# A hybrid streaming encoder on one core: a planner's table of durations is replaced, and the DeltaNet state update of two heads becomes one full-height matmul

## The chip, the cores and the metric

The kernel runs on one core of one Trainium2 chip. The metric is device time in microseconds (us) of one execution; smaller is better. The engines are named as in the profile: PE (TensorE matmul), PEld (its weight loads), DVE (VectorE), ACT (ScalarE), POOL (GpSimd), SP (SyncE, which issues the DMAs).

## What is computed

Two layers over 2048 prompt frames and 32 sample frames of width 1024. Layer 0 is sliding-window attention (16 query heads, 4 key heads, ALiBi, sinks). Layer 1 is a gated DeltaNet with 8 heads of 128 keys by 128 values, in chunks of 64 frames. Each layer has an input projection, a SiLU gate, an output projection and a residual; RMSNorm stands before each layer and at the end. The change touches the DeltaNet recurrence, which the reference writes as a scan over chunks:

```python
def step(s, xs):
    qi, ki, ui, wi, gi, ai = xs
    v_new = ui - jnp.einsum('bhcd,bhde->bhce', wi, s)
    o = jnp.einsum('bhcd,bhde->bhce', qi * jnp.exp(gi)[..., None], s) + jnp.einsum('bhij,bhje->bhie', ai, v_new)
    g_last = gi[..., -1]
    s = s * jnp.exp(g_last)[..., None, None] + jnp.einsum(
        'bhcd,bhce->bhde', ki * jnp.exp(g_last[..., None] - gi)[..., None], v_new)
    return s, o
```

## The kernel before, in words

**Tiling.** The tokens go through in four slabs of 512 (the second with the 32 sample frames, 544). Both projections are blocks of 24 matmuls (8 slices of the contraction by 3 products of a split into a high and a low part) into a PSUM bank `pj`; 512 columns at a time, or 272 for the slab of 544. They read activations `hk` and weights `wh`. In the profile they are the group pj<-hk,wh.

**The chain.** Heads are worked on in pairs, head x in the partitions of half x (64 frames of a chunk in each half). `chain_quad` (line 1635) does four chunks of a pair; 128 chunk steps for the prompt and 4 for the sample make 132. A step is a sequence over three engines, each part waiting for the one before:
- PE, two matmuls tb<-st,kq: keys and queries of each head times its state `st`;
- DVE, two scalar_tensor_tensor r<-tb,nbk,vb, one for each half; ACT scales the queries' part into `qs` after them, from the same bank;
- PE, tb<-r,btt: the inverse of the chunk's triangle times `r` (tb<-r,kqs in the last pair, and `kqs` stands for `kq` in the sample);
- ACT, a copy of the 128x128 result out of PSUM: `vn`, the new values of both heads, one head in each half of the partitions;
- PE, for each head a matmul of 64 rows, keys `kd` of its half times `vn` of its half, one into the bank tc and one into the free part of the bank tb; then tb<-vn,bit for the output;
- DVE, two scalar_tensor_tensor st<-st,egl: the decayed state plus the update; then `o`.
The next chunk of the pair needs the new `st`. So that PE has work meanwhile, projection matmuls of later blocks stand between the parts of a step.

**What sets the order.** Generators emit the program's operations; an object `Estimate` (line 77), with costs and lags of its own, decides when each generator goes on, so it sets the order of emission. Every operation is recorded by `Engine.made` (line 180; all instructions therefore have line 185 in the profile) with a rank, its place in the emission, less a lead for urgent ones (400 for evacuations of `pj`, 600 for the chain, line 220). Before the attention layer ends and at the program's end `Order.flush` (line 313) plans: it goes through time, and on each engine issues, of the operations that by its own account are ready, the one of lowest rank; if none is ready, the engine waits for the first that will be. An operation's cost there is the one from `Estimate.cost` (line 119), and the lag between engines is `Estimate.LAG` (line 82). The plan is no more than an order: on the chip each engine takes its instructions in that order, and waits where an input is late.

Of the kernel before, what the change touches and what calls it, by code (L numbers as in the profile page):

```python
# [12 lines left out]
F32R = mybir.dt.float32r  # L13
AF = mybir.ActivationFunctionType
ALU = mybir.AluOpType

P = 128
# [5 lines left out]
CH = 64  # L23
# [53 lines left out]
class Estimate:  # L77
# [4 lines left out]
    LAG = {  # L82
        "tensor": {"tensor": 0, "vector": 200, "scalar": 200, "gpsimd": 200},
        "vector": {"tensor": 256, "vector": 127, "scalar": 130, "gpsimd": 155},
        "scalar": {"tensor": 270, "vector": 145, "scalar": 34, "gpsimd": 160},
        "gpsimd": {"tensor": 200, "vector": 60, "scalar": 75, "gpsimd": 100},
    }
    MEAN = 200
# [82 lines left out]
class Engine:  # L171
# [5 lines left out]
    def __getattr__(self, op):  # L177
        call = getattr(self.engine, op)

        def made(*args, **kw):  # L180
            is_ap = lambda x: isinstance(x, bass.AP)
            outs = [x for x in ([] if "out" in kw else [args[0]]) + [kw.get("out"), kw.get("accum_out")] if is_ap(x)]
            ins = [x for x in list(args[0 if "out" in kw else 1 :]) + [v for k, v in kw.items() if k not in ("out", "accum_out")] if is_ap(x)]
            cost = self.est.note(self.name, op, outs, ins, kw)
            self.order.add(Op(self.name, lambda: call(*args, **kw), cost, op == "dma_start"), ins, outs)  # L185

        return made

# [7 lines left out]
class Op:  # L196


    def __init__(self, engine, call=None, cost=0.0, dma=False):
        self.engine, self.call, self.cost, self.dma = engine, call, cost, dma  # L200
        self.after, self.left, self.ends, self.done, self.rank = [], 0, {}, False, 0
        self.gang = None


class Place:
# [6 lines left out]
class Order:  # L212
# [15 lines left out]
    @contextmanager  # L228
    def together(self):

        self.gang = Op(None)
        self.ops.append(self.gang)
        yield
        self.gang = None

    def place(self, pool, tag, bufs, name):
        ring = self.rings.setdefault((id(pool), tag), [])
# [57 lines left out]
    def settle(self, op):  # L295

        if op.engine:
            lag = lambda by: self.est.LAG.get(by, {}).get(op.engine, self.est.MEAN)
            heapq.heappush(self.wait[op.engine], (max([end + lag(by) for by, end in op.ends.items()] + [0.0]), op.rank, op))
        else:  # L300
            self.finish(op)
# [11 lines left out]
    def flush(self):  # L313

        overs = []
        for p in self.places.values():
            if p.old and p.over is None:
                p.over = Op(None)
                overs.append(p.over)
                for o in p.old.ops:  # L320
                    self.link(o, p.over)
                for o in {id(o): o for o in p.ops}.values():
                    self.link(p.over, o)
                    if o.gang:
                        self.link(p.over, o.gang)
        self.wait = {e: [] for e in self.ENGINES}
        ready = {e: [] for e in self.ENGINES}
        for o in [o for o in overs + self.ops if o.left == 0]:
            self.settle(o)
        while any(self.wait.values()) or any(ready.values()):  # L330
            when = {e: max(self.free[e], 0.0 if ready[e] else self.wait[e][0][0]) for e in self.ENGINES if ready[e] or self.wait[e]}
            e = min(when, key=when.get)
            now = when[e]
            while self.wait[e] and self.wait[e][0][0] <= now:
                _, rank, o = heapq.heappop(self.wait[e])
                heapq.heappush(ready[e], (rank, o))
            _, op = heapq.heappop(ready[e])
            op.call()
            if op.dma:
                self.free[e] = now + 60  # L340
                self.dma = max(now + 1500, self.dma) + op.cost * (self.CLOSE if now < self.START else 1)
                op.ends = {"dma": self.dma + 500}
            else:
                self.free[e] = now + op.cost
                op.ends = {e: self.free[e]}
            op.start = now
            self.finish(op)
        assert all(o.done for o in self.ops)
        self.ops = []
# [49 lines left out]
class Kern:  # L399
# [848 lines left out]
    def delta_setup(self, bp):  # L1248
        nc = self.nc
        self.bp = bp  # L1250
        one = lambda shape, tag, dt=F32: self.t(bp, shape, tag, dt, bufs=1)
        self.st = one([P, DNH, P], "st")
        self.hist = one([P, 24, 3], "hist")
        nc.gpsimd.memset(self.hist, 0.0)
        self.hsmp = one([P, 24, 3], "hsmp")
        nc.sync.dma_start(self.hsmp, self.io["cv"])
        self.csmp = one([P, 24, 3], "csmp")

        self.cw = one([P, 96], "cw")
        nc.vector.tensor_scalar(out=self.cw, in0=self.par[:, PC_CW : PC_CW + 96], scalar1=0.5, scalar2=None, op0=ALU.mult)  # L1260
        self.dg = one([P, 1], "dgn")
        nc.vector.tensor_scalar(out=self.dg, in0=self.par[:, PC_DG : PC_DG + 1], scalar1=0.5, scalar2=None, op0=ALU.mult)
        self.na_ = one([P, 4], "na")
        nc.scalar.activation(self.na_, self.par[:, PC_AL : PC_AL + 4], AF.Exp)
        nc.vector.tensor_scalar(out=self.na_, in0=self.na_, scalar1=-1.0, scalar2=None, op0=ALU.mult)

        self.tts = [one([P, 4, P], f"btt{i}") for i in range(2)]
        self.its = [one([P, 4, P], f"bit{i}") for i in range(4)]

        def zeros():  # L1270
            for x in (*self.its, *self.tts, self.st):
                nc.gpsimd.memset(x, 0.0)
                yield 1000

        self.spawn(zeros(), "zeros", 5000)
        self.npair = self.nconv = 0
        self.chained, self.order, self.quads, self.had = set(), [], [], [None, None]
# [357 lines left out]
    def chain_quad(self, q, tab, off, states, gated, put):  # L1635
# [10 lines left out]
        for c in range(m):  # L1646
            state = yield from states(c)
            p1 = yield from self.bank("tb")
            self.issue.lead = Order.CHAIN
            for x in range(2):  # L1650
                self.mm(p1[:, x * P : (x + 1) * P], kq[:, c, x, :], state[:, x, :], True, True)
            r = self.t(bp, [P, P], f"r{q['i']}", bufs=1)
            qs = self.t(bp, [P, P], f"qs{q['i']}", bufs=1)
            half = [slice(y * CH, (y + 1) * CH) for y in range(2)]
            for x, rows in enumerate(half):
                nc.vector.scalar_tensor_tensor(
                    out=r[rows], in0=p1[rows, x * P : (x + 1) * P], scalar=q["nbk"][rows, c : c + 1], in1=q["vb"][rows, c, :],
                    op0=ALU.mult, op1=ALU.add)
            for x, rows in enumerate(half[::-1]):
                nc.scalar.activation(  # L1660
                    qs[rows], p1[rows, x * P : (x + 1) * P], AF.Identity, scale=tab["egq"][rows, off + c : off + c + 1])
            self.give("tb")
            self.issue.lead = 0
            yield
            p2 = yield from self.bank("tb")
            self.issue.lead = Order.CHAIN
            self.mm(p2[:, 0:P], q["tt"][:, c, :], r, True, True)
            vn = self.t(bp, [P, P], f"vn{q['i']}", bufs=1)
            nc.scalar.copy(vn, p2[:, 0:P])
            self.issue.lead = 0  # L1670
            yield

            p3 = yield from self.bank("tc")
            up = [p3[:, 0:P], p2[:, 2 * P : 3 * P]]
            self.issue.lead = Order.CHAIN
            for x in range(2):
                rows = slice(x * CH, (x + 1) * CH)
                self.mm(up[x], q["kd"][rows, c, :], vn[rows], True, True)
            self.mm(p2[:, P : 2 * P], q["it"][:, c, :], vn, True, True)
            for x in range(2):  # L1680
                nc.vector.scalar_tensor_tensor(
                    out=state[:, x, :], in0=state[:, x, :], scalar=tab["egl"][:, x, off + c : off + c + 1],
                    in1=up[x], op0=ALU.mult, op1=ALU.add)
            tt(out=o[:, c, :], in0=p2[:, P : 2 * P], in1=qs, op=ALU.add)
            self.issue.lead = 0
            self.give("tb")
            self.give("tc")
            yield
            nc.scalar.activation(qs, o[:, c, :], AF.Square, accum_out=so[:, c : c + 1])
            states.done(c)  # L1690
# [562 lines left out]
```

## Time and profile before

| what | value |
|---|---|
| median of 3 runs | 2374.01 us (2365.21 to 2376.85) |
| the profiled execution's own time | 2376.4 us |
| its span in the profile | 2374.6 us |
| mean granted clock of PE | 0.978 |
| PE busy / idle in the span | 2252.8 us / 121.8 us |
| first and last matmul of the chain's kind tb<-st,kq | 1039.8 us, 2343.3 us |

A busy share is the time in which at least one instruction of the engine ran. Matmuls overlap in the profile: a row of a merged group has its first start and its total length, so PE's pace is read from the starts of rows that follow each other. An fp32 matmul shows as two records (passes) of the same shape. In a list of waits, "A <- B" is time in which A was idle and B's result ended the idle time. A granted clock under 1 means that PE ran at that share of its full pace.

### The profile page before, as it was taken

The numbers are of one execution on the slowest core, as the hardware profiler recorded it, in microseconds if no ns is written. First come the engines' busy times: TensorE is split into PE (matmuls) and PEld (weight loads), VectorE is DVE, ScalarE is ACT, GpSimd is POOL, SyncE is SP. The second block draws the span as 40 slices with busy tenths as digits, with TensorE's granted clock in tenths as the row PEclk, the third lists the DMA queues.
The fourth block names the chain that finished last, engine by engine and source line by source line (L and its number), as shares of the span: only waits on it lengthen the run. The fifth ranks groups of instructions, "written<-read, shape, count | busy, mean of one in ns | idle before, by whom it ended". The sixth has DMA issues, their size and how long they took to land.

```text
span 2374.6 us, 44457 instructions
## 1 busy us (share of the span) xinstructions
PE 2252.8 (95%) x14759; PEld 1843.9 (78%) x14759; DVE 1639.6 (69%) x5024; ACT 1262.2 (53%) x3792; POOL 862.9 (36%) x1044
## 2 busy tenths in 40 slices
PE   8998999999999999999999999989999999999997
PEld 5777788797778777777778788877798767777776
DVE  6765465626553445588887768889786888876876
ACT  5555466636553554455566354564644466445533
POOL 4556555665554334222322121331312222122222
PEclk9998999999999999999999999999999999999998
DMA  7556755585434115544423664333456634466442
GB/s 253 175 187 192 255 188 181 174 279 190 147 105 150 62 63 159 193 149 140 143 89 126 200 227 136 128 115 122 147 172 215 200 118 138 134 215 216 155 142 67
DMA packets 222832, 382.75 MB, mean 161 GB/s; under 512 B 29922, under 2 KB 45194, under 8 KB 222602
## 3 DMA queue, kind: packets, MB, share of 16 engines
q1 hardware_dynamic: 220154, 377.75, 49.4%
q8 instruction: 116, 1.90, 0.3%
q10 hardware_dynamic: 2448, 2.16, 0.3%
q14 instruction: 114, 0.93, 0.1%
HBM read 311.63 MB, written 68.19 MB: 160 GB/s over the span
## 4 chain that ended last, share of the span: by engine, by line
PE 56%; DVE 28%; ACT 7%; issue 4%; DMA 3%; POOL 2%; SPq 0%; DVEq 0%; ACTq 0%; POOLq 0%
PE pj L185 39%; PE tb L185 6%; PE ta L185 5%; PE tc L185 4%; DVE cy L185 4%; DVE s L185 3%; DVE sub L185 3%; DVE tl L185 3%; ACT s L185 2%; DVE ml L185 2%; ACT ta L185 1%; DVE xa L185 1%; DVE r L185 1%; DVE md L185 1%; DVE mx L185 1%
## 5 line engine op out<-in xcount | busy, mean ns | idle before, releaser
L185 PE MATMUL pj<-hk,wh 128*128 128x512 f32 (+1 forms) x8184 | 1770.1, 364 | 26.9 <-DVE xr L185 8.6
L185 PEld LDWEIGHTS pj<-hk,wh 128*128 128x128 f32 x8184 | 1326.6, 191 | 237.9 <-issue 14.1
L185 POOL TENSOR_TENSOR wh<-wr,wh 128x512 fp32r<-128x512 f32 x224 | 295.5, 1321 | 328.2 <-ACT wh L185 283.7
L185 DVE SCALAR_TENSOR_TENSOR cy<-cx,cw,cy 128x512 f32<-128x512 f32 x360 | 230.6, 651 | 44.7 <-ACT cy L185 41.1
L185 ACT CAST wh<-wr 128x512 fp32r<-128x512 f32 x224 | 138.1, 618 | 203.6 <-PE pj L185 157.3
L185 ACT ACTIVATE s<-s,mx 128x256 f32<-128x256 f32 (+1 forms) x272 | 132.0, 487 | 30.1 <-DVE mx L185 29.9
L185 ACT ACTIVATE qs<-tb,egq 64x128 f32<-64x128 f32 x264 | 95.7, 362 | 89.7 <-DVE r L185 76.5
L185 DVE TENSOR_TENSOR sub<-ml,tl 128x60 f32<-128x60 f32 (+24 forms) x527 | 125.8, 239 | 10.2
L185 DVE TENSOR_SCALAR s<-s,den 128x256 f32<-128x256 f32 (+1 forms) x272 | 130.9, 530 | 1.2
L185 ACT ACTIVATE cx<-cy 128x512 f32<-128x512 f32 (+1 forms) x96 | 61.1, 636 | 130.9 <-DVE cy L185 101.5
L185 DVE TENSOR_TENSOR tl<-tl,sub 128x60 f32<-128x60 f32 (+24 forms) x527 | 122.3, 232 | 10.1
L185 DVE CUSTOM_DVE_ANT_0 s<-ta,bias 128x256 f32<-128x256 f32 (+1 forms) x272 | 95.7, 405 | 43.5 <-PE ta L185 42.9
L185 POOL TENSOR_TENSOR pr<-pr,ph 128x512 fp32r<-128x512 f32 x82 | 111.8, 1364 | 34.9 <-ACT ph L185 28.8
L185 POOL COPY cx<-hist 128x3 f32<-128x3 f32 x96 | 25.5, 265 | 263.9 <-DVE kq L185 63.6
L185 DVE TENSOR_TENSOR xr<-pj,xr 128x512 f32<-128x512 f32 (+1 forms) x72 | 41.2, 577 | 112.1 <-PE pj L185 70.1
L185 POOL TENSOR_TENSOR so<-so,mhalf 128x4 f32<-128x4 f32 x33 | 36.8, 1115 | 216.9 <-DVE so L185 189.1
L185 DVE SCALAR_TENSOR_TENSOR r<-tb,nbk,vb 64x128 f32<-64x128 f32 x264 | 91.7, 348 | 29.6 <-PE tb L185 25.1
L185 ACT ACTIVATE qs<-o 128x128 f32<-128x128 f32 x132 | 40.7, 308 | 133.8 <-DVE o L185 128.3
L185 ACT COPY cx<-pj 128x512 f32<-128x512 f32 (+2 forms) x149 | 64.1, 445 | 77.5 <-PE pj L185 62.1
L185 PE MATMUL tb<-st,kq 128*128 128x128 f32 x512 | 94.7, 286 | 6.8 <-DVE st L185 5.9
L185 PEld LDWEIGHTS tb<-st,kq 128*128 128x128 f32 x512 | 82.9, 194 | 21.5 <-DVE st L185 13.0
L185 PE MATMUL tb<-con,s 128*128 128x128 f32 (+2 forms) x528 | 77.7, 280 | 18.9 <-DVE s L185 16.0
(242 smaller groups left out, 3558.0 us busy)
## 6 DMA issues: line engine op xcount, KB each, us to landing
wh<-xswwd SPq DMA_DIRECT2D x528, 256.0 KB
wr<-in_wa SPq DMA_DIRECT2D x160, 256.0 KB
wh<-xswwdo SPq DMA_DIRECT2D x112, 256.0 KB
pr<-in_wd SPq DMA_DIRECT2D x66, 256.0 KB
xswwd<-ph SPq DMA_DIRECT2D x66, 256.0 KB
xswwd<-pr SPq DMA_DIRECT2D x66, 256.0 KB
wr<-in_wao SPq DMA_DIRECT2D x64, 256.0 KB
xa<-in_x SPq DMA_DIRECT2D x48, 256.0 KB
```

Source lines behind the costliest of these rows:

```text
L185: self.order.add(Op(self.name, lambda: call(*args, **kw), cost, op == "dma_start"), ins, outs)
```

## The change

Two things are changed.

**Another table in the planner.** `Order.measure` gives every operation other than a DMA its own cost for the plan: for DVE 150 ns and 1.05 ns a column (0.55 for copies and tensor_scalar within SBUF) in place of 68 and 1.04 (0.52), for ACT 148 and 0.845 in place of 52 and 0.83, for POOL 180 and 2.17 in place of 140 and 2.14, and more for scalar operands and accumulations. PE's projection matmuls cost 0.4375 ns a column and 7 ns in place of 1/2.4 and 3. The plan adds 100 ns where PE goes over to matmuls of another number of rows or columns (rounded up to 32, 64 or 128), and up to 300 ns to a DVE operation within SBUF while POOL is at work. Lags are new too, for example DVE to PE 120 ns in place of 256, DVE to DVE 20 in place of 127, PE to DVE or ACT 205 in place of 200. `Estimate`, and so the order of emission, keeps its own table. Only the order on the engines comes out otherwise.

**The state update.** Two tiles `vz` of [128, 2, 128] are zeroed once. In each step ACT copies each half of the result into its own block of `vz` (two copies of 64x128), and then `vn` as before. One matmul of 128 rows, `kd` of both heads times the 256 columns of `vz`, replaces the two of 64 rows; the zeros keep each head's keys from the other head's values. Its 256 columns all go into the bank tc.

```diff
+    TOOK = {"vector": (150, 1.05, 62), "scalar": (148, 0.845, 100), "gpsimd": (180, 2.17, 0)}
+    SWITCH, SHARED = 100, 300
+    def measure(self, new, op, outs, ins, kw):
...
+        new.cost = fixed + each * n
...
-            lag = lambda by: self.est.LAG.get(by, {}).get(op.engine, self.est.MEAN)
+            lag = lambda by: self.LAG.get(by, {}).get(op.engine, self.MEAN)
...
-                self.free[e] = now + op.cost
+                cost = op.cost
+                if e == "tensor":
+                    cost, tile = cost + (self.SWITCH if op.tile != tile else 0), op.tile
+                elif op.shares:
+                    cost += min(self.SHARED, max(0.0, self.free["gpsimd"] - now))
+                self.free[e] = now + cost
...
+        self.vz = [one([P, 2, P], f"vz{i}") for i in range(2)]
...
             vn = self.t(bp, [P, P], f"vn{q['i']}", bufs=1)
+            vz = self.vz[q["i"]]
+            for x, rows in enumerate(half):
+                nc.scalar.copy(vz[rows, x, :], p2[rows, 0:P])
             nc.scalar.copy(vn, p2[:, 0:P])
...
-            up = [p3[:, 0:P], p2[:, 2 * P : 3 * P]]
+            up = [p3[:, x * P : (x + 1) * P] for x in range(2)]
             self.issue.lead = Order.CHAIN
-            for x in range(2):
-                rows = slice(x * CH, (x + 1) * CH)
-                self.mm(up[x], q["kd"][rows, c, :], vn[rows], True, True)
+            self.mm(p3[:, 0 : 2 * P], q["kd"][:, c, :], vz.rearrange("p x d -> p (x d)"), True, True)
             self.mm(p2[:, P : 2 * P], q["it"][:, c, :], vn, True, True)
```

Where instructions move is seen at three places. First PE, before, in the chain of the second pair of heads in the first slab of the DeltaNet layer, from the second chunk's r matmul on (`con` is the identity of a transpose, ta<-con,kq belongs to the next pair's preparation; all numbers are buffer numbers):

```order
L185 MATMUL tb_11605<-r_2601_11591,btt_2207_11197 128x128
L185 MATMUL ta_11622<-con_112,kq_11526 128x128 x4
L185 MATMUL pj_11614<-hk_2452,wh_11588 128x512
L185 MATMUL tc_11609<-vn_2616_11606,kd_11409 128x128
L185 MATMUL tb_11605<-vn_2616_11606,kd_11409 128x128
L185 MATMUL tb_11605<-vn_2616_11606,bit_2211_11201 128x128
L185 MATMUL pj_11614<-hk_2452,wh_11588 128x512
L185 MATMUL pj_11614<-hk_2452,wh_11589 128x512
L185 MATMUL tb_11615<-st_11190,kq_11350 128x128
L185 MATMUL pj_11632<-hk_2414,wh_11612 128x512
L185 MATMUL tb_11615<-st_11190,kq_11350 128x128
L185 MATMUL ta_11624<-con_112,kq_11542 128x128 x4
```

Projection matmuls of two blocks (pj_11614, pj_11632) stand between the parts of the step.

PE after the change, at the same chunk of the same pair:

```order
L185 MATMUL tb_11607<-r_2615_11605,btt_2207_11197 128x128
L185 MATMUL tc_11616<-vz_2213_11203,kd_11411 128x256
L185 MATMUL tb_11607<-vn_2618_11608,bit_2211_11201 128x128
L185 MATMUL ta_11624<-con_112,kq_11514 128x128 x4
L185 MATMUL tb_11617<-st_11190,kq_11352 128x128 x2
L185 MATMUL tb_11622<-r_2628_11618,btt_2207_11197 128x128
L185 MATMUL ta_11626<-con_112,kq_11544 128x128 x4
L185 MATMUL tc_11625<-vz_2213_11203,kd_11411 128x256
L185 MATMUL tb_11622<-vn_2633_11623,bit_2211_11201 128x128
L185 MATMUL tb_11627<-st_11190,kq_11352 128x128 x2
L185 MATMUL tb_11635<-r_2638_11628,btt_2207_11197 128x128
```

From the second chunk's r matmul to the fourth's there is no projection matmul; transposes of the next pair's keys are all that stands between the parts of the chain. It goes on like this to the pair's eighth r matmul.

On ACT, before, at the same step (`qs` is the queries' part; the rows with `sx` are sums of squares for the next pair):

```order
L185 ACTIVATE qs_2602_11592<-tb_11590,egq_11226 64x128 x2
L185 COPY vn_2616_11606<-tb_11605 128x128
L185 ACTIVATE ta_11604,sx_11601<-ta_11604 128x128
L185 COPY kd_11598<-ta_11622 64x512
L185 ACTIVATE ta_11604,sx_11601<-ta_11604 128x128
```

And after the change:

```order
L185 ACTIVATE qs_2616_11606<-tb_11604,egq_11228 64x128 x2
L185 COPY vz_2213_11203<-tb_11607 64x128 x2
L185 COPY vn_2618_11608<-tb_11607 128x128
L185 ACTIVATE ta_11598,sx_11595<-ta_11598 128x128
L185 ACTIVATE ta_11603,sx_11600<-ta_11603 128x128 x2
```

The two half copies into `vz` stand ahead of the copy of `vn`, and all three read the bank that the r matmul wrote.

More of the change, by code (lines that the diff above doesn't have):

```diff
@@ L184, in made @@
             cost = self.est.note(self.name, op, outs, ins, kw)
-            self.order.add(Op(self.name, lambda: call(*args, **kw), cost, op == "dma_start"), ins, outs)
+            new = Op(self.name, lambda: call(*args, **kw), cost, op == "dma_start")
+            if not new.dma:
+                self.order.measure(new, op, outs, ins, kw)
+            self.order.add(new, ins, outs)
         return made
@@ L201, in __init__ @@
         self.after, self.left, self.ends, self.done, self.rank = [], 0, {}, False, 0
-        self.gang = None
+        self.gang, self.tile, self.shares = None, None, False
 class Place:
@@ L234, in together @@
         self.gang = None
+    TOOK = {"vector": (150, 1.05, 62), "scalar": (148, 0.845, 100), "gpsimd": (180, 2.17, 0)}
+    LAG = {
+        "tensor": {"tensor": 0, "vector": 205, "scalar": 205, "gpsimd": 230},
+        "vector": {"tensor": 120, "vector": 20, "scalar": 60, "gpsimd": 90},
+        "scalar": {"tensor": 120, "vector": 45, "scalar": 20, "gpsimd": 80},
+        "gpsimd": {"tensor": 120, "vector": 40, "scalar": 40, "gpsimd": 80},
+    }
+    MEAN = 200
+    SWITCH, SHARED = 100, 300
+    def measure(self, new, op, outs, ins, kw):
+        size = lambda x: x.free_size() if callable(x.free_size) else x.free_size
+        out, near = outs[0], all(x.space == bass.MemoryType.SB for x in [*outs, *ins])
+        if new.engine == "tensor":
+            k, m, n = ins[0].shape[0], out.shape[0], size(out)
+            up = lambda n: 32 if n <= 32 else 64 if n <= 64 else 128
+            new.tile = up(k), up(m)
+            if op == "transpose":
+                new.cost = 109.0
+            elif ins[0].dtype == F32R:
+                new.cost = max(107.0, 0.4375 * n + 7) * (0.53 if k == CH else 1)
+            else:
+                new.cost = max(216.0, 4 * n / 2.4 + 4) * {32: 0.2, 64: 0.52}.get(m, 1)
+            return
+        n = max(size(x) for x in [*outs[:1], *ins])
+        fixed, each, more = self.TOOK[new.engine]
+        if op == "transpose":
+            fixed, each = 190, 1.8
+        if new.engine == "gpsimd" and op == "tensor_copy":
+            each = 3.3
+        if new.engine == "vector":
+            if near and op in ("tensor_copy", "tensor_scalar"):
+                each = 0.55
+            new.shares = near
+        if new.engine == "scalar" and ins[0].space == bass.MemoryType.SB:
+            fixed += 50
+        new.cost = fixed + each * n
+        if any(isinstance(kw.get(k), bass.AP) for k in ("scale", "bias", "scalar", "scalar1")):
+            new.cost += more
+        if "accum_out" in kw:
+            new.cost += 188 if new.engine == "scalar" else 82
+        if kw.get("op") == ALU.pow:
+            new.cost += 185 * n + 70
     def place(self, pool, tag, bufs, name):
@@ L327, in flush @@
         ready = {e: [] for e in self.ENGINES}
+        tile = None
         for o in [o for o in overs + self.ops if o.left == 0]:
@@ L1268, in delta_setup @@
         self.its = [one([P, 4, P], f"bit{i}") for i in range(4)]
+        self.vz = [one([P, 2, P], f"vz{i}") for i in range(2)]
         def zeros():
-            for x in (*self.its, *self.tts, self.st):
+            for x in (*self.its, *self.vz, *self.tts, self.st):
                 nc.gpsimd.memset(x, 0.0)
```

## The prediction, on record before the changed kernel ran

> **What bounds the kernel now.** The page first: its span, the busy engines, and the chain that ended last.
>
> ```profile
> span 2374.6 us, 44457 instructions
> PE 2252.8 (95%) x14759; PEld 1843.9 (78%) x14759; DVE 1639.6 (69%) x5024; ACT 1262.2 (53%) x3792; POOL 862.9 (36%) x1044
> PE 56%; DVE 28%; ACT 7%; issue 4%; DMA 3%; POOL 2%; SPq 0%; DVEq 0%; ACTq 0%; POOLq 0%
> ```
>
> PE is busy for 95% and holds over half of the chain; the next link is DVE. The kernel ends when PE has run all its matmuls and has waited wherever its order ran into a late input. So the change is worth what it does to two sums: PE's work, and PE's idle time, 2374.6 - 2252.8 = 121.8 us. The windows answer gives the DeltaNet stage (from 1040 us) and one stretch of it:
>
> ```profile
> 1040.00:2374.60 1334.60, 1263.22 (x8447) 1040.75 (x8445) 1054.86 (x3322) 707.16 (x2335) 338.06 (x564) 0.97 0.47 151
> 2303.00:2320.60 17.60, 15.22 (x116) 10.96 (x115) 9.01 (x30) 7.03 (x24) 1.58 (x2) 0.68 0.05 15
> ```
>
> After span and PE the columns are PEld, DVE, ACT, POOL and then PE's granted clock. In the stage DVE is busy for 1054.86 of 1334.60 us (79%), ACT for 53%. The second row is the one long place where PE's order has no projection matmul; its clock falls to 0.68. Then the list of who PE waited for (total, times, longest):
>
> ```profile
> PE tb L185 <- DVE s L185: 16.0, 20, 2.5
> PE tb L185 <- DVE r L185: 13.3, 12, 3.7
> PE pj L185 <- DVE xr L185: 8.6, 7, 2.0
> PE tb L185 <- DVE st L185: 5.9, 9, 1.8
> PE pj L185 <- ACT cy L185: 4.5, 6, 2.0
> PE tc L185 <- ACT vn L185: 2.7, 5, 1.4
> ```
>
> The attention layer's softmax costs PE 16.0 us, the chain 13.3 + 5.9 + 2.7 = 21.9 us. No wait is large; the kernel loses in small pieces that an order could take away.
>
> **The state update on PE.** The timeline of PE around a chunk step that runs amid projection matmuls:
>
> ```profile
> 1824.98 0.38 PE L185 MATMUL tb<-r,btt 128*128 128x128 f32 x2
> 1825.12 0.94 PE L185 MATMUL pj<-hk,wh 128*128 128x512 f32 x3
> 1825.99 0.37 PE L185 MATMUL tc<-vn,kd 64*128 64x128 f32 x1
> 1826.00 0.37 PE L185 MATMUL tb<-vn,kd 64*128 64x128 f32 x1
> 1826.20 0.27 PE L185 MATMUL tc<-vn,kd 64*128 64x128 f32 x1
> 1826.21 0.27 PE L185 MATMUL tb<-vn,kd 64*128 64x128 f32 x1
> 1826.41 0.49 PE L185 MATMUL tb<-vn,bit 128*128 128x128 f32 x2
> 1826.66 1.40 PE L185 MATMUL pj<-hk,wh 128*128 128x512 f32 x5
> 1827.90 0.61 PE L185 MATMUL tb<-st,kq 128*128 128x128 f32 x4
> 1828.26 1.64 PE L185 MATMUL pj<-hk,wh 128*128 128x512 f32 x6
> 1829.73 0.38 PE L185 MATMUL tb<-r,btt 128*128 128x128 f32 x2
> 1829.87 0.48 PE L185 MATMUL pj<-hk,wh 128*128 128x512 f32 x1
> ```
>
> A projection matmul of 512 columns advances PE by (1.64 - 0.48) / 5 = 0.232 us. From 1827.90 to 1829.73, less six of these (1.39), four fp32 passes took 0.44, so a full-height fp32 matmul of 128 columns (two passes) costs about 0.215. From 1824.98 to 1827.90 there are 2.92 us: eight projection matmuls (1.86), the r matmul (0.215), and so 0.845 for the update and the output matmul, 0.63 for the two updates alone. The rows show why: the heads' matmuls start 0.01 apart, but the second passes come 0.21 later, twice the 0.11 of a full-height pass, and 0.17 is lost on the way in (1825.99 - 1825.12 - 3 x 0.232). The new matmul has 256 columns and full height. No such fp32 row stands there amid projection matmuls; the nearest are the one of 128 columns (0.215, so 0.43 for twice the columns) and one of 512:
>
> ```profile
> L185 PE MATMUL ms<-rb,ones x2: 592/592/592, 25.8 to 26.2; 128*128 128x512 f32 x2
> ```
>
> Its passes start 0.4 apart, which is 0.2 for 256 columns and 0.4 for both passes. I take 0.43: 0.63 - 0.43 = 0.20 saved, by 132 steps **-26 us** (bounds -13, if half of the loss on the way in stays, and -30 by the row of 512).
>
> The Trainium skill, TensorEngine Tiling (Array Packing), Overview (Theoretical Speedup), speaks against this edit: two tiles of 64 rows should give up to twice the speed, so that the pair would cost one matmul. The start 0.01 apart agrees with tiles that run side by side, the 0.21 to the next pass doesn't. The same page, Tiling Modes (Key Properties), says that a change of mode drains the array, which agrees with the 0.17.
>
> **The copies on ACT.** Two more copies a step, 264 in all.
>
> ```profile
> L185 ACT COPY vn<-tb 128x128 f32<-128x128 f32 x132 | 33.4, 253 | 21.9 <-PE tb L185 21.0 <-DVE trc L185 0.4
> L185 DVE SCALAR_TENSOR_TENSOR r<-tb,nbk,vb 64x128 f32<-64x128 f32 x264 | 91.7, 348 | 29.6 <-PE tb L185 25.1
> L185 ACT COPY kd<-ta 64x512 f32<-64x512 f32 x66 | 37.0, 578 | 8.5 <-PE ta L185 7.8
> ```
>
> The nearest rows are `vn` itself (253 ns at 128 columns) and a copy of 64 rows and 512 columns (578), so height doesn't make one cheap: 264 x 0.253 = 67 us of ACT, from 707 to 774 us of the stage (58%). As throughput that is hidden behind PE. As latency it isn't: the update waits for both half copies in place of one full copy, so a step's cycle grows by 0.25 us. Queued behind them on ACT are `vn` (the output matmul waits 0.5 us longer, off the state's cycle) and evacuations of `pj`. At the program's end the last eight steps have no cover: 8 x 0.25 = **+2 us** (0 to +8).
>
> **The order around the chain.** How fast can a step follow the last? Two r matmuls in the fastest pair, then three in the stretch at 2303:
>
> ```profile
> 1343.43 0.46 PE L185 MATMUL tb<-r,btt 128*128 128x128 f32 x2 [0.37 <-DVE btt L185]
> ...
> 1347.58 0.38 PE L185 MATMUL tb<-r,btt 128*128 128x128 f32 x2
> ```
> ```profile
> 2308.57 0.49 PE L185 MATMUL tb<-r,btt 128*128 128x128 f32 x2 [0.57 <-DVE r L185]
> 2312.99 0.80 PE L185 MATMUL tb<-r,kqs 128*128 128x128 f32 x2 [0.90 <-DVE r L185]
> 2317.78 0.79 PE L185 MATMUL tb<-r,kqs 128*128 128x128 f32 x2
> ```
>
> 4.15 us at full clock, 4.42 and 4.79 in the stretch. Of the 4.15 a step's own matmuls fill 0.215 + 0.845 + 0.43 = 1.49; the rest, 2.66 us, is eleven projection matmuls, or idle. So I counted, in the order of each kernel, the work that stands on PE between successive r matmuls, each matmul at its price from rows like the above. Before, 4 of 131 gaps hold under 3 us and 3 hold no projection matmul; after, 21 and 12. Set against 4.15, the shortfalls before sum to 14 us; the waits measured 21.9, so the count is of the right size and low. Set against 4.15 + 0.25 = 4.40, those after sum to 54 us. The difference from the measured 21.9 is **+32 us** (from +23 with a cycle 0.25 shorter, to +40 against the count before). The largest piece is the second pair of the first slab, where six gaps of 1.3 to 2.5 us stand in a row: 6 x 4.40 = 26.4 us of chain over 12.6 us of work.
>
> Bare stretches also pull the clock. In the 17.6 us at 0.68 the four steps' own work, 4 x 1.49 = 6 us, takes 6 x (1 / 0.68 - 1) = 2.8 us longer. For one longer stretch and some short ones I take **+6 us** (0 to +15). The Trainium skill, TensorE: Matmul & The Clock Gate (What's actually happening), puts the clock at half after an idle window of some 3.4 us; the 0.68 agrees, and by an all-half stretch the second pair's 12.6 us of work would cost 12.6 more.
>
> **The order elsewhere.** The plan now prices an r of 128 columns at 150 + 1.05 x 128 + 62 = 346 ns (the row: 348) where it had 68 + 1.04 x 128 + 60 = 261, so what waits for DVE and ACT is put later. In the attention layer the projection matmuls between a softmax tile's scores and its transposes rise from 30 to 36 (medians over 72 tiles), 6 x 0.232 = 1.4 us at most. The 20 waits for `s` have a mean of 0.8 and a longest of 2.5, so most of the 16.0 goes: **-14 us** (0 to -16). Of the projection's own waits for DVE and ACT (8.6 and 4.5 among them) I take **-9 us** (-18 to +10, as the same backlog on DVE, 79% busy, meets projections that now stand bunched). SP's DMAs keep their costs in the plan; none of the waits quoted is for a DMA.
>
> **Sum.** -26 + 2 + 32 + 6 - 14 - 9 = -9 us on the profiled execution's own 2376.4 us (span 2374.6 and 1.8 around it): 2367.4. It ran 2.4 above the median of the runs shown, 2374.0, so 2365; I say **2366 us**, -0.3%. About 0.5% (2362 to 2386) is what a measurement can tell here from no change.
>
> **The rivals.**
> - *The new order wins.* The chain's cycle in a bunch, with DVE and ACT less disturbed, is about 3.9 before the copies, so the chain's term is +23; the softmax waits go wholly (-16), the projection's -18, and no clock is lost. -26 - 16 - 18 + 23 = -37: 2337 us. For it: the table's 346 against 348. Against it: the 21 thin gaps, which nothing can fill, since PE takes its queue in order.
> - *The bare chain costs more than the drains.* In the bunches PE and DVE idle together; what they held back, convolutions of the next blocks, then comes in a rush on a DVE that is 79% busy, and projections wait for it. Chain +40, clock +15, projection waits +10, softmax only -5, copies +2, update -26: +36, 2410 us. It decides once PE's idle time grows by over 26 us, which the update saves. For it: 4.42 and 4.79 at 2303. Against it: nowhere in the trace of before do such stretches have projections waiting long behind them.
> - *Two half-height matmuls are the cheaper form.* If the pair is as good as one (0.215) once nothing else disturbs it, the new one adds 0.215 x 132 = 28 where I have -26: +54 on the sum, 2420 us. The 0.21 between passes speaks against it. This is the Trainium skill's rule from TensorEngine Tiling (Array Packing) above.
> - *The change does not do what it says.* The order moves, but what is late stays late: the update's -26 alone, 2348 us.
>
> **How the numbers follow.** The balance of the sum 0.40, with a range of its own of 2348 to 2386; the order wins 0.24; the bare chain 0.26; the half-height form 0.04; the update alone 0.06. Faster: 0.23 + 0.05 + 0.15 of the balance = 0.43. Slower: 0.26 + 0.04 + 0.03 = 0.33. Within 0.5%: the rest, 0.24. The unknown costs at their better ends give -30 - 16 + 23 - 18 = -41 (2333), at their worse ends -13 + 8 + 40 + 15 + 10 = +60 (2434); of the second I leave out the last part, of the first I take in some more for cases of the first rival that go further: 2325 to 2420.
>
> **What would show it.** Right: the group tc<-vz,kd with starts 0.43 apart from the next matmul amid projections; 264 copies `vz` near 0.25 us; PE's waits for `r`, `st` and the half copies up from 21.9 to about 50 us, most of it in the second pair of the first slab; PE's wait for `s` under 5 us. Wrong: the new matmul at 0.6 or more; chain waits that stay near 20 us although the gaps are thin (a cycle far below 4.4); or projection waits in the DeltaNet stage that grow by over 20 us.

## The result and the profile after

The changed kernel takes 2426.06 us (median of 4 runs, 2424.07 to 2426.74), the kernel before beside it 2372.28 (4 runs): a ratio of 1.0228, 95% interval 1.0201 to 1.0255. It is 54 us slower, where 2366 us was forecast with a range that ended at 2420. The profiled execution took 2425.66 us, at a mean granted clock of 0.958 (before 0.978). Its page:

```profile
span 2423.8 us, 44180 instructions
PE 2255.5 (93%) x14495; PEld 1880.4 (78%) x14495; DVE 1625.0 (67%) x5024; ACT 1336.7 (55%) x4056; POOL 868.0 (36%) x1046
PE 81%; DVE 9%; ACT 3%; DMA 2%; issue 2%; POOL 1%; SPq 0%; DVEq 0%; ACTq 0%; POOLq 0%
```

PE's busy time hardly differs (2252.8 before). What has grown is its idle time, 2423.8 - 2255.5 = 168.3 us against 121.8: 46.5 of the span's 49.2 us. The growth is all in the DeltaNet stage; the attention layer's last softmax transpose even starts 10 us earlier (896.2 us, before 906.5). The windows answer for that stage, with the columns as in the prediction, and for two stretches of it:

```profile
1040.00:2423.80 1383.80, 1253.27 (x8133) 1062.85 (x8131) 1040.68 (x3313) 772.96 (x2591) 347.88 (x563) 0.94 0.46 144
1140.20:1178.70 38.50, 24.07 (x135) 18.17 (x133) 27.55 (x99) 28.72 (x115) 7.38 (x10) 0.90 0.07 21
1261.40:1274.20 12.80, 2.62 (x16) 1.62 (x14) 12.23 (x58) 6.38 (x19) 5.63 (x7) 0.70 0.16 51
```

The stage is 49 us longer and its clock went from 0.97 to 0.94. The second row is the bare second pair of the first slab, which the prediction named. The third it did not see: for 12.8 us PE does next to nothing while DVE is full. Next, who PE waited for (total, times, longest). First come three rows of before that the prediction did not use:

```profile
PE ta L185 <- DVE tq L185: 4.9, 9, 1.8
PE ta L185 <- ACT o L185: 3.2, 3, 2.4
PE ms L185 <- DVE g L185: 1.4, 3, 0.7
```

And from the list after the change (the three dots stand for rows left out):

```profile
PE ta L185 <- ACT o L185: 20.0, 9, 5.5
PE pj L185 <- ACT cy L185: 18.4, 8, 6.7
PE tb L185 <- DVE r L185: 14.3, 19, 1.1
PE tc L185 <- ACT vz L185: 13.9, 23, 1.0
PE ms L185 <- DVE g L185: 12.3, 3, 7.2
PE ta L185 <- DVE tq L185: 11.8, 5, 5.7
PE tb L185 <- DVE s L185: 9.6, 12, 2.5
...
PE tb L185 <- DVE st L185: 5.3, 13, 1.8
```

The chain's waits (r, vz, st) are 33.5 us, 11.6 more than the 21.9 of before. The softmax (s) gave back 6.4. But four others, few and long, grew by 16.8 (o), 13.9 (cy), 10.9 (g) and 6.9 (tq): 48.5 us together. They are waits for what DVE and ACT had yet to do. One of the four is a wait of projection matmuls (`cy`); `o` and `tq` are waits of transposes, and `g` is one of the gates' matmul. All the waits of projection matmuls for DVE and ACT went from 24.2 to 38.1 us. PE's timeline through the stretch at 1261 shows two of the four kinds, `g` and `cy`:

```profile
1261.19 0.50 PE L185 MATMUL pj<-hk,wh 128*128 128x272 f32 x2
1265.18 1.08 PE L185 MATMUL ms<-g,con 128*128 128x36 f32 x8 [3.50 <-DVE g L185]
1266.10 1.21 PE L185 MATMUL ta<-con,o 128*128 128x128 f32 x4
1267.10 0.42 PE L185 MATMUL ms<-con,gc 128*36 128x128 f32 x1
1274.24 1.04 PE L185 MATMUL pj<-hk,wh 128*128 128x272 f32 x3 [6.72 <-ACT cy L185]
```

The gates' matmul waits 3.50 us for DVE, and the projection behind it 6.72 us more. No projection matmul starts for 12 us. Over the whole trace (worked out from the starts of pj<-hk,wh) such holes of over 5 us sum to 202.7 us after and 60.6 before; PE has other work in part of them. So the order holds projections back, and PE has less to do while DVE and ACT catch up.

### The profile page after: what moved, and what is told of

Its sections match the earlier page's. It is cut to its first block, busy times and chain, and to the rows that moved or that the text cites. A ratio compares the mean times of both kernels' runs of the same rounds, so it can differ in the third digit from the quotient of the medians.

```text
span 2423.8 us, 44180 instructions
## 1 busy us (share of the span) xinstructions
PE 2255.5 (93%) x14495; PEld 1880.4 (78%) x14495; DVE 1625.0 (67%) x5024; ACT 1336.7 (55%) x4056; POOL 868.0 (36%) x1046
## 4 chain that ended last, share of the span: by engine, by line
PE 81%; DVE 9%; ACT 3%; DMA 2%; issue 2%; POOL 1%; SPq 0%; DVEq 0%; ACTq 0%; POOLq 0%
PE pj L185 60%; PE ta L185 8%; PE tb L185 7%; PE tc L185 5%; PE ms L185 1%; DVE tl L185 1%; DVE sub L185 1%; DVE s L185 1%; DVE xa L185 1%; DVE r L185 1%; ACT qs L185 1%; DVE hk L185 1%; DVE st L185 0%; DMA xr<-in_x 0%; DMA xa<-xsx 0%
## 5 line engine op out<-in xcount | busy, mean ns | idle before, releaser
L185 PE MATMUL pj<-hk,wh 128*128 128x512 f32 (+1 forms) x8184 | 1752.5, 364 | 42.5 <-ACT cy L185 18.4
L185 DVE SCALAR_TENSOR_TENSOR cy<-cx,cw,cy 128x512 f32<-128x512 f32 x360 | 238.9, 670 | 49.4 <-ACT cy L185 46.1
L185 ACT COPY cx<-pj 128x512 f32<-128x512 f32 (+3 forms) x149 | 64.9, 452 | 146.5 <-PE pj L185 102.3
L185 DVE SCALAR_TENSOR_TENSOR st<-st,egl,tc 128x128 f32<-128x128 f32 x256 | 77.5, 344 | 98.8 <-PE tc L185 97.2
L185 DVE TENSOR_TENSOR tl<-tl,sub 128x60 f32<-128x60 f32 (+24 forms) x527 | 129.7, 246 | 7.2
L185 DVE TENSOR_SCALAR s<-s,den 128x256 f32<-128x256 f32 (+1 forms) x272 | 119.1, 493 | 2.0
L185 POOL TENSOR_TENSOR ss<-ss,mhalf 128x8 f32<-128x8 f32 x33 | 55.6, 1686 | 175.9 <-DVE ss L185 175.8
L185 POOL TENSOR_TENSOR pr<-pr,ph 128x512 fp32r<-128x512 f32 x82 | 108.4, 1323 | 26.4 <-ACT ph L185 25.4
L185 POOL COPY hist<-cx 128x3 f32<-128x3 f32 x96 | 21.2, 221 | 225.7 <-ACT cx L185 225.0
L185 POOL COPY cx<-hist 128x3 f32<-128x3 f32 x96 | 35.5, 371 | 185.3 <-DVE kq L185 62.3
```

The lines of the kernel that those rows point to most:

```text
L185: new = Op(self.name, lambda: call(*args, **kw), cost, op == "dma_start")
```

## The experiments

The theories, as the expectations name them. **D**: the new table gives a DVE, ACT or POOL instruction its length in the profile, as the time for which it holds its engine. The next instruction starts before that length is over, so the plan believes these engines fuller than they are, lets PE run the chain bare (with no projection matmul between its parts) and holds projections back. **C**: the longer step is to blame, by the two copies and the bare chain, whatever the table. **S**: the two surcharges, for PE's change of shape and for DVE beside POOL, distort the plan. **E** and **L** are for the update alone: its copies shift the order of emission, or cost by themselves. For D there were these rows of DVE's timeline in the trace of before:

```profile
1817.79 0.35 DVE L185 SCALAR_TENSOR_TENSOR st<-st,egl,tb 128x128 f32<-128x128 f32 x1
1818.06 0.28 DVE L185 TENSOR_TENSOR o<-tb,qs 128x128 f32<-128x128 f32 x1
```

The row `st` is 0.35 us long, and the next starts 0.27 after it, 0.08 before its end. Over all pairs in which the next instruction waits for nothing, it starts about 83 ns before the end on DVE, 95 to 100 on ACT and 42 to 45 on POOL: `st` holds DVE for 259 ns of 343, a convolution `cy` of 512 columns for 663 of 746, a copy of 128 columns ACT for 145 of 247. The old table has 261, 660 and 158 for these three. It was never too low; it priced the pace. The Trainium skill, Perfetto Trace Analysis (Per-instruction lifecycle, DVE / Act Engine Instruction), says as much: the row ends when the write is acknowledged, and the next instruction may begin its reads once the first has finished executing. The trace agrees.

**One part at a time: vz_alone and table_alone.** The first is the kernel before with the new state update; the second the changed kernel with the old one.

```diff
+++ vz_alone
...
+            for x, rows in enumerate(half):
+                nc.scalar.copy(vz[rows, x, :], p2[rows, 0:P])
...
-                self.mm(up[x], q["kd"][rows, c, :], vn[rows], True, True)
+            self.mm(p3[:, 0 : 2 * P], q["kd"][:, c, :], vz.rearrange("p x d -> p (x d)"), True, True)
```

table_alone has the same lines turned round.

> The kernel before with the state update as one full-height matmul, its order planned with the old table. Theory D (the new table takes an instruction's length for the time it holds its engine, and the bad order is the whole loss): about 2350 us, the 20 to 26 us that the matmul saves on PE. Theory C (the two extra copies lengthen every chunk step and that is the loss): 2400 us or more. Theory S (the planner's two surcharges are the loss): as D, 2350.

> The changed kernel with the old state update (two half-height matmuls, one copy), order planned with the new table. Theory D and theory S: slower than the changed kernel, 2430 to 2450 us, since the saving on PE is gone and the table stays. Theory C: 2375 us or less.

vz_alone: 2384.17 us, ratio 1.0038 (1.0024 to 1.0051). table_alone: 2445.45, 1.0295 (1.027 to 1.032). The loss is the table's. The update is worth about 19 us within the table's order, and in the old order it is 9 us slower, less than C's loss and without the gain of 26. C falls as the cause: table_alone has no extra copy and loses the most.

**The table mended: pitch, and no_surcharges.** In pitch the plan frees an engine before the instruction's end by the overlap; results are still due at the end.

```diff
+++ pitch
+    TAIL = {"vector": 83, "scalar": 100, "gpsimd": 45}
...
-                self.free[e] = now + cost
-                op.ends = {e: self.free[e]}
+                self.free[e] = now + cost - self.TAIL.get(e, 0)
+                op.ends = {e: now + cost}
+++ no_surcharges
-    SWITCH, SHARED = 100, 300
+    SWITCH, SHARED = 0, 0
```

> The changed kernel, but in the plan an engine is free 83 ns (DVE), 100 ns (ACT) or 45 ns (POOL) before its instruction's result is there, as the trace of before shows them to overlap (a state update on DVE is 343 ns long, and the next instruction starts 259 ns after it). The same lengths, lags and surcharges otherwise. Theory D: the thin gaps between chunk steps go, and the time falls to 2340 to 2365 us. Theory S and theory C: it stays within 15 us of the changed kernel's 2426.

> The changed kernel with both surcharges of the plan at zero (100 ns at a change of tile shape on PE, up to 300 ns for DVE beside POOL), lengths and lags as changed. Theory S: 2365 us or less. Theory D: 2390 to 2420 us, since the surcharges only add to an engine load that is already put too high. Theory C: 2426.

pitch: 2351.82 us, 0.9893 (0.9862 to 0.9925), 74 us below the changed kernel with all else the same, and below the kernel before. no_surcharges: 2410.26, 1.0144 (1.0118 to 1.017). D's forecast came true, and S explains 16 of the 54 us at most. PE's timeline in pitch, second pair of the first slab, where the changed kernel is bare:

```profile
1144.05 0.38 PE L185 MATMUL tb<-r,btt 128*128 128x128 f32 x2
1144.18 1.40 PE L185 MATMUL pj<-hk,wh 128*128 128x512 f32 x5
1145.42 0.59 PE L185 MATMUL tc<-vz,kd 128*128 128x256 f32 x2
1145.86 0.38 PE L185 MATMUL tb<-vn,bit 128*128 128x128 f32 x2
1146.00 2.11 PE L185 MATMUL pj<-hk,wh 128*128 128x512 f32 x8
1148.16 0.75 PE L185 MATMUL tb<-st,kq 128*128 128x128 f32 x4
```

Thirteen projection matmuls stand within the step. Thin gaps between r matmuls, counted as in the prediction, are 4 of 131 in pitch, 21 in the changed kernel, 13 in table_alone. Holes of over 5 us without a projection matmul sum to 53.5 us. From the list of PE's waits in pitch:

```profile
PE ta L185 <- DVE tq L185: 14.6, 9, 4.8
PE tb L185 <- DVE r L185: 7.5, 11, 2.1
PE ta L185 <- ACT o L185: 7.2, 5, 5.1
...
PE pj L185 <- ACT cy L185: 4.3, 3, 1.9
PE tc L185 <- ACT vz L185: 4.2, 9, 1.2
...
PE ms L185 <- DVE g L185: 3.0, 2, 1.5
```

Of the four waits that grew, `o`, `cy` and `g` fall back; `tq` does not, it is the longest that is left. The new lags and the new costs of PE stay in pitch, which beats the kernel before, so the loss is not theirs; they were not tried alone.

**Which engine's tail: pitch_dve and pitch_act.** Two experiments with one engine's overlap alone (POOL's at 0).

```diff
+++ pitch_dve
+    TAIL = {"vector": 83, "scalar": 0, "gpsimd": 0}
+++ pitch_act
+    TAIL = {"vector": 0, "scalar": 100, "gpsimd": 0}
```

> As the run pitch, but only DVE is free before its result is there (83 ns); ACT and POOL hold their engine for the whole length. Theory D with the weight on DVE, the busier engine: 2355 to 2375 us, most of the 74 us from 2426 to 2352. If DVE and ACT count alike: near 2390.

> As the run pitch, but only ACT is free before its result is there (100 ns). Theory D with the weight on DVE: 2400 to 2420 us, since 14 of the thin gaps between chunk steps stay. If DVE and ACT count alike: near 2390.

pitch_dve: 2372.55, 0.9988 (0.9973 to 1.0003). pitch_act: 2425.17, 1.0212 (1.0193 to 1.0232). DVE's 83 ns alone bring 54 of the 74 us. ACT's alone bring nothing, less than the 6 to 26 us expected. The last 20 came only with all three, and are little more than the chance that the next runs show.

**Is it the chance of one order? after_plus3, after_minus3, pitch_plus3, pitch_minus3.** A plan is one draw: any small shift gives another. These move every fixed cost of DVE, ACT and POOL by 3 ns, in the changed kernel and in pitch.

```diff
+++ after_plus3, pitch_plus3
+    TOOK = {"vector": (153, 1.05, 62), "scalar": (151, 0.845, 100), "gpsimd": (183, 2.17, 0)}
+++ after_minus3, pitch_minus3
+    TOOK = {"vector": (147, 1.05, 62), "scalar": (145, 0.845, 100), "gpsimd": (177, 2.17, 0)}
```

> The changed kernel with 3 ns more in each length of the plan's table for DVE, ACT and POOL, which means nothing on the chip. If lengths taken for occupancy are the loss: 2410 to 2445 us, like the four runs that keep them for DVE. If the loss of the changed kernel was one unlucky order: anywhere, below 2390 too.

> The same with 3 ns less: 2410 to 2445 us if lengths taken for occupancy are the loss; anywhere if it was luck.

> The run pitch with 3 ns more in each length. If the corrected occupancy is the gain: 2335 to 2370 us. The distance from 2352 is the chance part that any edit brings, by which the runs copy_more (2335) and pitch_no_surcharges (2397) are to be read.

> The same with 3 ns less: 2335 to 2370 us if the corrected occupancy is the gain.

after_plus3 2433.42 (1.0239, 1.0216 to 1.0261), after_minus3 2416.09 (1.0172, 1.0157 to 1.0187); pitch_plus3 2353.92 (0.9914, 0.9897 to 0.993), pitch_minus3 2346.55 (0.988, 0.9866 to 0.9895). Three orders with lengths take 2416 to 2433, three with the overlap 2347 to 2354. The families stay 62 us apart at the nearest, so the cause is the table's meaning: a length used as the time for which an engine is held. Within a family the orders lie 7 and 17 us apart by chance, and below that no single run says much. The waits go with it. In the six kernels whose plan prices DVE by length (the changed kernel, its two shifts, table_alone, no_surcharges, pitch_act), PE's waits for `o`, `cy`, `g` and `tq` sum to 47 to 74 us, and the holes without a projection matmul to 179 to 220 us. In the other fourteen kernels of this document, they are 14 to 39 and 39 to 102 us. The chain's waits do not go with it: table_alone, the slowest, has 14.6 us of them, less than the 21.9 of before.

**Where the update's gain goes: vz_quiet, pitch_two_halves, vn_first, copy_more, split.** vz_quiet is vz_alone with the copies left out of `Estimate`, so that emission is hardly shifted. The others start from pitch: the old two matmuls; `vn` copied ahead of the halves, which makes a step's cycle another 0.25 us longer; one more, useless copy a step on ACT; the second half copied on DVE.

```diff
+++ vz_quiet
...
+            unseen = outs[0].tensor.name.startswith("vz") and op != "memset"
+            cost = 158.0 if unseen else self.est.note(self.name, op, outs, ins, kw)
...
+++ pitch_two_halves
...
+                self.mm(up[x], q["kd"][rows, c, :], vn[rows], True, True)
...
+++ vn_first
             vz = self.vz[q["i"]]
+            nc.scalar.copy(vn, p2[:, 0:P])
             for x, rows in enumerate(half):
                 nc.scalar.copy(vz[rows, x, :], p2[rows, 0:P])
-            nc.scalar.copy(vn, p2[:, 0:P])
+++ copy_more
+            vx = self.t(bp, [P, P], f"vx{q['i']}", bufs=1)
+            nc.scalar.copy(vx, vn)
+++ split
-            for x, rows in enumerate(half):
-                nc.scalar.copy(vz[rows, x, :], p2[rows, 0:P])
+            nc.scalar.copy(vz[half[0], 0, :], p2[half[0], 0:P])
+            nc.vector.tensor_copy(vz[half[1], 1, :], p2[half[1], 0:P])
```

> The kernel before with the state update as one full-height matmul and the old table, as in the run vz_alone, but the two half copies are left out of the account that decides the order of emission (the plan still gives each 158 ns), so that the program is emitted almost as before. Theory E (in vz_alone the matmul's 25 us were lost again because the emission, and with it every rank, shifted): 2350 to 2360 us. Theory L (they were lost to the copies themselves, in ACT's queue and in each step's cycle): it stays at 2375 to 2390.

> The run pitch with the old state update (two half-height matmuls, one copy). If the full-height matmul keeps its saving on PE in a good order: 2370 to 2380 us, 20 to 26 above the run pitch. If the extra copies take it back, as they seem to in vz_alone: 2340 to 2355.

> The run pitch with the copy of vn ahead of the two half copies, so that the state update waits 0.25 us longer in each of the 132 steps and ACT does the same work. If the lengthened cycle is what takes the matmul's saving back: 2365 to 2385 us (up to 132 x 0.25 = 33 more). If it is ACT's load or nothing but the order: within 10 us of the run pitch's 2352.

> The run pitch with one more 128x128 copy of vn on ACT in each step, into a tile that nothing reads, behind the three that are there: 132 x 0.25 = 33 us more of ACT work, none of it waited for. If ACT's load takes the saving back: 2362 us or more. If not: within 10 us of 2352.

> The run pitch with the second half copy on DVE, beside the first on ACT: the cycle is about as long as with one copy, ACT has 33 us less and DVE some 26 us more. If cycle or ACT's load takes the saving back: 2325 to 2342 us. If neither: within 10 us of 2352.

vz_quiet 2369.57 (0.9982, 0.9966 to 0.9998), between the ranges of E and L: the shift of emission was 15 us of vz_alone, and without it the update gains 4 of its 26 (both within or near the chance of one order, so neither theory is shown). pitch_two_halves 2355.91 (0.9919, 0.9898 to 0.9941): in a good order too the update is worth about 4 us. vn_first 2354.42 (0.9918, 0.9892 to 0.9945) and split 2351.12 (0.9898, 0.9861 to 0.9936) are pitch's time, so neither the length of a step nor the load of two copies on ACT takes the gain. copy_more is the fastest kernel of all, 2335.08 (0.9836, 0.9805 to 0.9866), with a copy that does no useful work. It is 17 us below pitch, as far as the orders of the changed kernel lie apart. Its four executions had a granted clock of 0.980 to 0.982, those of pitch 0.973 to 0.979; the difference of the means, 0.0055 of 2340 us, is 13 of the 17 us, an estimate. Why this order keeps the clock up was not found, and a lucky order is the likeliest. That more work on ACT is no loss is all that it shows. The pages show where the gain goes, first pitch:

```profile
span 2353.2 us, 44132 instructions
PE 2249.6 (96%) x14495; PEld 1863.7 (79%) x14495; DVE 1623.0 (69%) x5024; ACT 1331.8 (57%) x4056; POOL 873.3 (37%) x1046
```

Then pitch_two_halves:

```profile
span 2355.2 us, 44484 instructions
PE 2266.7 (96%) x14759; PEld 1848.3 (78%) x14759; DVE 1621.9 (69%) x5024; ACT 1266.1 (54%) x3792; POOL 864.4 (37%) x1044
```

PE is busy for 17 us less with the new update and idle for 15 us more (103.6 against 88.5). In the other two pairs of orders PE's idle time grows by much the same: 15.9 us from before to vz_alone (121.8 to 137.7), 16.6 from table_alone to the changed kernel (151.7 to 168.3). It looks as if PE gets to the same late inputs sooner; which input that is each time was not settled. PE's busy time does not fall evenly in the three pairs: by 2.4 us from before to vz_alone, 38.6 from table_alone to the changed kernel, and 17.1 here, while the granted clock goes from 0.978 to 0.973, 0.951 to 0.958, and 0.976 to 0.973. So the clock takes part of the update's saving, or adds to it, as the order falls out.

**The surcharges in the mended plan: pitch_no_surcharges, pitch_no_share, pitch_no_switch.**

```diff
-    SWITCH, SHARED = 100, 300
+++ pitch_no_surcharges
+    SWITCH, SHARED = 0, 0
+++ pitch_no_share
+    SWITCH, SHARED = 100, 0
+++ pitch_no_switch
+    SWITCH, SHARED = 0, 300
```

> The run pitch with both surcharges of the plan at zero. If they describe the chip (a drain at a change of tile shape, DVE slower beside POOL): 2355 to 2375 us, slower than pitch. If they overprice as the lengths did: 2335 to 2350.

> The run pitch without the surcharge for DVE beside POOL (up to 300 ns), the one for a change of tile shape kept. The two together were worth 45 us (2397 against 2352), four times the chance part of some 10. If the share of DVE beside POOL is what they describe: 2380 to 2400 us here and 2345 to 2365 without the other one. If it is the drain of PE: the other way round.

> The run pitch without the 100 ns for a change of tile shape on PE, the surcharge for DVE beside POOL kept. If the drain of PE is what makes the 45 us: 2380 to 2400 us. If DVE beside POOL makes them: 2345 to 2365.

2396.98 (1.0099, 1.0068 to 1.0129), 2383.64 (1.0027, 1.0016 to 1.0039) and 2354.38 (0.9904, 0.9888 to 0.9921). The first lies above both of its expected ranges. In the mended plan the price of DVE beside POOL is worth 32 us; the price of PE's change of shape nothing by itself. With lengths as costs, taking both away helped by 16 us, no more than the chance of one order; mended, it costs 45. That the surcharge harms only where DVE is overpriced already fits D, but was not tried by itself.

## Why the prediction was wrong, point by point

**The step that failed** is "The order elsewhere". It took the plan's 346 ns for an `r`, against the row's 348, as the sign that the plan knows DVE's time, "so what waits for DVE and ACT is put later", at -14 and -9 us. The row's length is right for when the result is there and wrong for when DVE is free: over DVE's 5024 instructions 83 ns each are up to 417 us that the plan adds to an engine whose busy time is 1625 us. So in the plan DVE falls behind, and projections and transposes are put where it believes that their inputs and banks come free. How this leads to each hole on the chip is inferred, since no run keeps the plan's own times; that it does, pitch shows, which undoes this one thing and is 74 us faster. Of the term's two parts, the softmax gave 6.4 of its 14. The projections' own waits, put at -9 with a worst end of +10, grew by 14. And the waits of transposes and gates (`o`, `g`, `tq`), which had no term at all, grew by 34.6.

**The state update, -26.** As a cost on PE it was right. PE's timeline after the change, amid projections:

```profile
1854.77 1.41 PE L185 MATMUL pj<-hk,wh 128*128 128x512 f32 x5
1856.01 0.59 PE L185 MATMUL tc<-vz,kd 128*128 128x256 f32 x2
1856.44 0.38 PE L185 MATMUL tb<-vn,bit 128*128 128x128 f32 x2
```

And the group of the copies:

```profile
L185 ACT COPY vz<-tb 64x128 f32<-64x128 f32 x264 | 67.9, 257 | 33.5 <-PE tb L185 30.8
```

1856.44 - 1856.01 = 0.43, the value taken. The rival of two half-height matmuls falls. As a term of the time it was too large: 19 us within the table's order, 4 in pitch, a loss in vz_alone, and only the first of these lies above the 7 to 17 us of chance. The forecast took work saved on PE for time saved, with PE 95% busy; 15 to 17 us of it came back as idle time.

**The copies, +2.** 257 ns against 253, and vn_first, with a cycle longer again, takes pitch's time. From the start of the last projection matmul to the end of the span are 43.6 us after the change and 35.3 before, 37.4 in pitch and 34.3 in pitch_two_halves: within the term's range or just beyond it.

**The order around the chain, +32.** The place was right, the size not. Rows of the bare pair, with its second, third and eighth r matmul:

```profile
1143.33 0.49 PE L185 MATMUL tb<-r,btt 128*128 128x128 f32 x2 [1.02 <-DVE r L185]
1144.58 0.70 PE L185 MATMUL tc<-vz,kd 128*128 128x256 f32 x2 [0.76 <-ACT vz L185]
...
1147.28 0.49 PE L185 MATMUL tb<-r,btt 128*128 128x128 f32 x2 [0.81 <-DVE r L185]
...
1170.94 0.76 PE L185 MATMUL tb<-r,btt 128*128 128x128 f32 x2 [0.81 <-DVE r L185]
```

The first of these steps takes 3.95 us, less than the 4.15 of before and the 4.40 assumed, even with one copy more in it. But the six gaps that the prediction priced at 26.4 us take 1170.94 - 1143.33 = 27.61, so the pair itself came out as forecast. Its steps hold 11.1 us of waits for `r`, `vz` and `st` (the whole pair, in PE's timeline). That leaves 22.4 us for all the rest of the kernel, where before had 21.9 in all: the other thin gaps, counted as the larger part of the 54 us, brought next to no more waits of the chain. In all they rose by 11.6 us.

**The clock, +6.** The mean went from 0.978 to 0.958; (1 - clock) x span goes from 52 to 102 us, which bounds this term by +50. PE's busy time gives a nearer figure: it rose by 2.7 us although the update took work away, 26 by the term above, so some 29 us of it is slower running, an estimate (20, if the 17 us of pitch and pitch_two_halves are the work taken away). Holes like the one at 1261 (0.70) were not in the term. The bare second pair had 0.90, so it was not a stretch at half the clock, and the 12.6 us named for that case did not come there. pitch does the same work at 0.973 to 0.979, so the lost clock comes with the order; its own share was not tried apart.

**The rivals.** "The bare chain costs more than the drains" has the sign and 2410 us, and its condition, PE idle for over 26 us more, came true with 46.5. It also named the waits for convolutions, and `cy` is one. That its time is near is in part luck: its sum put +40 on the chain and +10 on the projections' waits, which were 12 and 14, and had nothing for the 35 of transposes and gates. The chance of 0.26 for it was too small: the 21 thin gaps, in which the plan let PE stand idle of its own choice, were seen and not asked about.

## What to carry to other kernels

When a plan's costs are set from a profile, take from a run of instructions that wait for nothing the spacing of their starts for how long an engine is held, and the row's length only for when the result is there; the two differ by a fixed amount per instruction. Before trusting a new table, compare what the plan gives to what it already ran: an old number that seems too low may be the right one of another quantity. And judge such an order by several small shifts of its costs, since orders that differ by such a shift alone lie 7 to 17 us apart here.

## What the runs showed of the hardware

- Rows overlap on each engine: the next instruction starts about 83 ns before the end on DVE, 95 to 100 on ACT, 42 to 45 on POOL, as medians over the trace of before.
- DVE beside POOL. The group of the softmax's scaling in before has a mean far from its usual length:

```profile
L185 DVE TENSOR_SCALAR s<-s,den 128x256 f32<-128x256 f32 x240 | 116.9, 536 | 1.0
```

Of these, 146 that ran with POOL idle have a median of 347 ns, 73 that shared over half of their time with it 1353. An `r`, which reads PSUM, has means of 348 and 347 in the same two cases. The Trainium skill, SBUF — State Buffer (Who interferes with whom), says that such an instruction can be shut out for the whole of POOL's; the numbers agree, and pricing it is worth 32 us of a plan.
- The fp32 update of 64 rows a head cost 0.63 us of PE for the pair, the full-height matmul with zeros 0.43, and the time of the kernel moved for it by anything from 19 us less (in the changed plan) to 9 us more (in the plan of before).
